# Row pair two in seven products in the first feed-forward block of a two-layer trunk

## The chip, the cores and the metric

The kernel runs on one core of one Trainium2 chip. The metric is device time in microseconds of one execution, as a median over runs; "the profiled execution" is a single one of them, taken by the hardware profiler.

## The reference

A decoder trunk of two layers works on 256 tokens of 2048 features in fp32. Layer 0 mixes tokens with a chunkwise mLSTM, layer 1 with a Griffin recurrent block; after each mixer stands a feed-forward part, which alone is touched here:

```python
def swiglu(x, w_in, w_out):
    g, u = jnp.split(x @ w_in, 2, axis=-1)
    return (jax.nn.silu(g) * u) @ w_out
...
        h = h + mix
        h = h + swiglu(rms_norm(h, norm_ffn[layer]), ffn_w_in[layer], ffn_w_out[layer])
    return rms_norm(h, norm_final)
```

`w_in` is 2048 x 11264 (gate and up halves of 5632 columns each), `w_out` is 5632 x 2048.

## The kernel before, in words

**Precision.** An fp32 matrix is split into an upper part (a cast to fp32r on ACT, `whi` for weights) and a lower part (raw minus upper on DVE, `wlo`). A product of two matrices is three matmuls, upper by upper, upper by lower and lower by upper (`product`, lines 821, 822 and 823). The names of the tiles carry the case: `whi`/`wlo` for a plain pair, `whix`/`wlox` and `whit`/`wlot` for one in seven products, `whio`/`wloo` for output weights, `p_f` and `m_f` for split activations.

**Tiling of the feed-forward part.** The columns of each half of `w_in` are taken in 11 blocks of 512 (`j` = 0 to 10, block one is `j` = 0). Within a block the 2048 rows of `w_in` are taken in 8 pairs of 128-row tiles (`p` = 0 to 7, so pair number two is `p` = 1). A pair makes a 2 x 2 problem: two token blocks of 128, two row tiles, and two column blocks (gate and up). It is done in one of two ways:

- plain: 8 products, into four PSUM banks named Q5, P2, Q3 and P4;
- in seven products of sums and differences (Strassen's scheme), into the same four banks and three more, P1, P7 and Q6. The weights' side then needs sums of the raw tiles first: `sum` at lines 314, 317 and 318, then the split of three raw tiles (`whix`, `wlox`) and of four sums (`whit`, `wlot`). The activations' side has its seven combinations ready in `p_f`.

Each bank sums over all pairs of the block. P1, P7 and Q6 get their last product at `p` = 6; then line 855 copies P1, line 856 subtracts that from Q6, and line 858 subtracts P7. After `p` = 7 lines 861 to 870 finish the block. The order of the seven products is P1, P2, Q3, Q5, P7, Q6, P4.

Which pairs are plain is said by three constants:

```python
SEVENS = (1, 2, 3, 4, 5, 6)
BOTH = (1, 2, 3, 4)
SECOND = (3,)
    def is_plain(j, p):
        return p not in SEVENS or j == 0 and p in BOTH or j == 1 and p in SECOND
```

**Activations.** `NormPairs.pair(p)` turns a pair of feature tiles of `h` by four transposes on PE (`tr_f`, line 467) into a bank that `misc` hands out, scales it on ACT into a tile `c` (line 471), takes differences on DVE (line 473 for `p` = 0 and 7, lines 477 to 480 for the others) and splits the result into `p_f`. A pair in `BOTH` is prepared for both ways: one copy (line 490), one difference (line 491) and one split into `m_f` more. Pairs 0 to 5 are prepared beside the output projection of the mixer. Pairs 6 and 7 are left over as pending work, and are run in block one after `p` = 0 and after `p` = 1:

```python
            if left == 0 and p < 2:
                run_pending()
```

In the feed-forward part `misc` takes the banks in turn, one buffer each: `misc=["P1", "Q6", "P7"]`. The `c` tiles of pairs 6 and 7 share one place, `raw0` of the pool `rawo`, with a raw tile of output weights.

**Buffers and queues.** Raw weights come by DMA on SP's queue (line 305, two loads of 512 KB for a pair) into three places in rotation, and `whi` and `wlo` have three places each; in block one the second raw tile and the second `whi` tile have an extra place. A planner orders the instructions of each engine ahead of time by priority and readiness; weight sums, splits and the work on finished banks are raised by `AHEAD` = 1000. A tile whose place is still held waits for the last reader of the tile before it. The products with `w_out` (`outs`) for a block are spread over the next one, so block one has none.

Of the kernel before, what the change touches and what calls it, by code (L numbers as in the profile page):

```python
# [28 lines left out]

SEVENS = (1, 2, 3, 4, 5, 6)  # L30

BOTH = (1, 2, 3, 4)

SECOND = (3,)

# [9 lines left out]
def kernel(  # L45
# [247 lines left out]
    def is_plain(j, p):  # L293
        return p not in SEVENS or j == 0 and p in BOTH or j == 1 and p in SECOND

# [157 lines left out]
    class NormPairs(Norm):  # L453
# [6 lines left out]
        def pair(self, p):  # L460
# [26 lines left out]
            self.x.append(xt)  # L487
            if p in BOTH:

# [721 lines left out]
```

## Time and profile before

| | |
|---|---|
| median of 3 runs | 2078.71 us (2077.93 to 2078.84) |
| profiled execution | 2078.14 us |
| its span | 2076.0 us |
| granted TensorE clock, mean | 0.999 |
| matmuls on PE | 10490 |
| moved from HBM | 401.84 MB |

Times in the profile count from the start of the span. PE is TensorE's matmuls and PEld its weight loads, DVE is VectorE, ACT is ScalarE, SP the queue that issues the DMAs. In rows of a timeline stand the start, the duration, engine, line, operation, output tile and input tiles with buffer numbers left out, and in brackets the idle time before it with what ended it. A `P` or `Q` as an output is one of the banks above. In rows of a table of stretches stand the busy times of PE, PEld, DVE, ACT and POOL with their counts of instructions, then the granted clock, the DMA engines' share and GB/s. Groups of instructions show total busy time, the mean in ns and the idle time before them. Block one of layer 0 runs from about 398 to 441 us, that of layer 1 982 us later.

### The profile page before, as it was taken

The numbers are of one execution on the slowest core, as the hardware profiler recorded it, in microseconds if no ns is written. First come the engines' busy times: TensorE is split into PE (matmuls) and PEld (weight loads), VectorE is DVE, ScalarE is ACT, GpSimd is POOL, SyncE is SP. The second block draws the span as 40 slices with busy tenths as digits, with TensorE's granted clock in tenths as the row PEclk, the third lists the DMA queues.
The fourth block names the chain that finished last, engine by engine and source line by source line (L and its number), as shares of the span: only waits on it lengthen the run. The fifth ranks groups of instructions, "written<-read, shape, count | busy, mean of one in ns | idle before, by whom it ended". The sixth has DMA issues, their size and how long they took to land.

```text
span 2076.0 us, 27538 instructions
## 1 busy us (share of the span) xinstructions
PE 2066.2 (100%) x10490; PEld 1755.4 (85%) x10490; DVE 1733.4 (83%) x1888; ACT 1343.1 (65%) x1623; POOL 43.3 (2%) x62
## 2 busy tenths in 40 slices
PE   9999999999999999999999999999999999999998
PEld 8988888888888888888889999888888888888886
DVE  6655556699999999999976787679999999999995
ACT  6345446566777677767764778556776776776774
POOL 0011110000000000000000000000000000000002
PEclk9999999999999999999999999999999999999999
DMA  7556656555665566665555666665666556566653
GB/s 229 172 159 178 181 177 227 185 199 190 210 214 197 186 222 203 203 213 196 182 180 159 191 190 185 218 215 183 203 213 213 202 187 210 199 209 211 203 191 133
DMA packets 211900, 405.74 MB, mean 195 GB/s; under 512 B 15080, under 2 KB 15800, under 8 KB 211640
## 3 DMA queue, kind: packets, MB, share of 16 engines
q1 hardware_dynamic: 211048, 402.92, 59.2%
q8 instruction: 82, 1.34, 0.3%
q10 hardware_dynamic: 720, 1.07, 0.2%
q14 instruction: 50, 0.41, 0.1%
HBM read 401.84 MB, written 2.10 MB: 195 GB/s over the span
## 4 chain that ended last, share of the span: by engine, by line
PE 96%; DVE 2%; ACT 1%; issue 1%; DMA 0%; POOL 0%; ACTq 0%; POOLq 0%; DVEq 0%
PE P L821 7%; PE out L821 7%; PE P L823 7%; PE P L822 7%; PE out L823 7%; PE out L822 7%; PE Q L821 6%; PE Q L822 6%; PE Q L823 6%; PE po L332 3%; PE po L330 3%; PE po L331 3%; PE v L330 1%; PE o L332 1%; PE v L331 1%; PE rec L349 1%
## 5 line engine op out<-in xcount | busy, mean ns | idle before, releaser
L246 DVE TENSOR_TENSOR wlo<-raw,whi 128x1024 fp32r<-128x1024 f32 (+1 forms) x226 | 273.4, 1213 | 171.4 <-ACT whi L245 168.9
L245 ACT CAST whi<-raw 128x1024 fp32r<-128x1024 f32 (+1 forms) x226 | 234.7, 1043 | 196.2 <-PE po L332 42.6
L270 ACT CAST whit<-sum 128x1024 fp32r<-128x1024 f32 x244 | 251.4, 1052 | 147.4 <-DVE sum L318 77.6
L271 DVE TENSOR_TENSOR wlot<-sum,whit 128x1024 fp32r<-128x1024 f32 x244 | 292.2, 1218 | 20.4 <-ACT whit L270 20.3
L821 PE MATMUL out<-whio,hh 128*128 128x512 f32 x704 | 274.9, 391 | 0.1
L822 PE MATMUL out<-wloo,hh 128*128 128x512 f32 x704 | 274.0, 389 | 0.0
L823 PE MATMUL out<-whio,hh 128*128 128x512 f32 x704 | 273.9, 389 | 0.0
L270 ACT CAST whio<-rawo 128x1024 fp32r<-128x1024 f32 (+1 forms) x166 | 183.6, 1106 | 61.8 <-PE out L823 52.8
L271 DVE TENSOR_TENSOR wlox<-raw,whix 128x1536 fp32r<-128x1536 f32 x122 | 213.7, 1751 | 10.7 <-ACT whix L270 10.6
L271 DVE TENSOR_TENSOR wloo<-rawo,whio 128x1024 fp32r<-128x1024 f32 (+1 forms) x166 | 209.6, 1281 | 3.1 <-ACT whio L270 2.7
L270 ACT CAST whix<-raw 128x1536 fp32r<-128x1536 f32 x122 | 181.0, 1484 | 33.8 <-DMA raw<-in_ffn_w_in_dram 18.9
L940 ACT COPY h<-out 128x512 f32<-128x512 f32 x154 | 90.1, 585 | 128.4 <-PE out L823 128.2
L821 PEld LDWEIGHTS out<-whio,hh 128*128 128x128 f32 x704 | 132.2, 188 | 29.3 <-ACT out L929 1.6
L314 DVE TENSOR_TENSOR sum<-raw 128x1024 f32<-128x1024 f32 x122 | 149.1, 1222 | 8.8 <-DMA raw<-in_ffn_w_in_dram 3.8
L823 PEld LDWEIGHTS out<-whio,hh 128*128 128x128 f32 x704 | 132.2, 188 | 27.6
L822 PEld LDWEIGHTS out<-wloo,hh 128*128 128x128 f32 x704 | 132.2, 188 | 27.1
L271 DVE TENSOR_TENSOR wlo<-raw,whi 128x2048 fp32r<-128x2048 f32 x54 | 122.0, 2288 | 30.0 <-ACT whi L270 30.0
L270 ACT CAST whi<-raw 128x2048 fp32r<-128x2048 f32 x54 | 101.2, 1913 | 18.0 <-DMA raw<-in_ffn_w_in_dram 17.8
L821 PE MATMUL P<-whix,p_f 128*128 128x512 f32 x244 | 96.6, 397 | 0.1
L929 ACT COPY out<-h 128x512 f32<-128x512 f32 x156 | 91.9, 589 | 6.4 <-DVE h L938 4.6
L822 PE MATMUL Q<-wlot,p_f 128*128 128x512 f32 x244 | 95.1, 390 | 0.0
L822 PE MATMUL P<-wlox,p_f 128*128 128x512 f32 x244 | 95.1, 390 | 0.0
(293 smaller groups left out, 5028.4 us busy)
## 6 DMA issues: line engine op xcount, KB each, us to landing
raw<-in_ffn_w_in_dram SPq DMA_DIRECT2D x352, 512.0 KB, 4.6
rawo<-in_ffn_w_out_dram SPq DMA_DIRECT2D x176, 512.0 KB, 4.8
raw<-in_m_w_in_dram SPq DMA_DIRECT2D x94, 512.0 KB, 3.8
raw<-in_r_w_in_dram SPq DMA_DIRECT2D x64, 512.0 KB, 4.2
raw<-in_m_w_out_dram SPq DMA_DIRECT2D x32, 512.0 KB, 3.7
raw<-in_r_w_out_dram SPq DMA_DIRECT2D x32, 512.0 KB, 4.4
gr<-in_r_gate_w_dram SPq DMA_DIRECT2D x8, 512.0 KB, 3.8
out_dram<-y SPq DMA_DIRECT2D x4, 512.0 KB, 3.0
```

The lines of the kernel that those rows point to most:

```text
L245: nc.scalar.copy(hi[:, i:i + step, 0:ncols], r)
L246: nc.vector.tensor_tensor(lo[:, i:i + step, 0:ncols], r, hi[:, i:i + step, 0:ncols].bitcast(F32), op=ALU.subtract)
L270: nc.scalar.copy(hi, src)
L271: nc.vector.tensor_tensor(lo, src, hi.bitcast(F32), op=ALU.subtract)
L314: nc.vector.tensor_tensor(t[:, 0:2, :], raw[:, 1:3, :], raw[:, 3:4, :].broadcast_to([P, 2, NB]), op=ALU.add)
L330: nc.tensor.matmul(o, lhsT=ah[:, bs], rhs=hi, start=(k == 0), stop=False)
L331: nc.tensor.matmul(o, lhsT=ah[:, bs], rhs=lo, start=False, stop=False)
L821: nc.tensor.matmul(o, lhsT=a[0], rhs=b[0], start=start, stop=False, **kw)
L822: nc.tensor.matmul(o, lhsT=a[0], rhs=b[1], start=False, stop=False, **kw)
L823: nc.tensor.matmul(o, lhsT=a[1], rhs=b[0], start=False, stop=stop, **kw)
L929: nc.scalar.copy(o, hs)
L940: nc.scalar.copy(hs, o)
```

## The change

`BOTH` loses its first entry. So in block one of each layer pair number two (`p` = 1) is taken in seven products, as it is in the other blocks, and `pair(1)` no longer prepares what the plain way needs.

```diff
 SEVENS = (1, 2, 3, 4, 5, 6)
 
-BOTH = (1, 2, 3, 4)
+BOTH = (2, 3, 4)
 
 SECOND = (3,)
```

## The prediction

> **What bounds the kernel now.** I read the page first: busy times, then the chain that ended last.
>
> ```profile
> span 2076.0 us, 27538 instructions
> PE 2066.2 (100%) x10490; PEld 1755.4 (85%) x10490; DVE 1733.4 (83%) x1888; ACT 1343.1 (65%) x1623; POOL 43.3 (2%) x62
> PE 96%; DVE 2%; ACT 1%; issue 1%; DMA 0%; POOL 0%; ACTq 0%; POOLq 0%; DVEq 0%
> ```
>
> PE has work in 2066.2 of 2076.0 us and is 96% of the chain. Fewer matmuls can pay; anything that makes PE wait costs its full length. Then the stretches around the first block of layer 0's feed-forward part (PE, PEld, DVE, ACT, POOL busy, granted clock), and one later in the layer:
>
> ```profile
> 404.00:410.00 6.00, 6.00 (x30) 4.92 (x30) 5.12 (x4) 4.47 (x5) 0.00 (x0) 1.00 0.55 193
> 436.00:441.00 5.00, 5.00 (x24) 4.14 (x23) 5.00 (x6) 2.97 (x3) 0.00 (x0) 1.00 0.90 304
> 1000.00:1060.00 60.00, 60.00 (x264) 49.11 (x263) 54.65 (x49) 43.54 (x48) 0.00 (x0) 1.00 0.55 182
> ```
>
> PE never stops, and DVE is full at the end of block one (5.00 of 5.00). The last row gives the price of a matmul on PE: 60.00 us / 264 = 0.227 us. (The 0.39 us of a single matmul overlaps with the next one.)
>
> **The change: PE work removed.** A plain pair takes 8 products, one in seven takes 7, and a product is 3 matmuls. So each layer loses 3 matmuls of 0.227 us, 0.68 us; both layers 1.36 us. That is 0.07% of 2078 us. It is the whole gain that is to be had: under 0.2%, about what a measurement of this kernel can tell from no change.
>
> **The weight side.** The pair's weights now need three sums and two splits instead of one split:
>
> ```profile
> L271 DVE TENSOR_TENSOR wlo<-raw,whi 128x2048 fp32r<-128x2048 f32 x54 | 122.0, 2288 | 30.0 <-ACT whi L270 30.0
> L270 ACT CAST whi<-raw 128x2048 fp32r<-128x2048 f32 x54 | 101.2, 1913 | 18.0 <-DMA raw<-in_ffn_w_in_dram 17.8 <-ACT whit L270 0.2
> L314 DVE TENSOR_TENSOR sum<-raw 128x1024 f32<-128x1024 f32 x122 | 149.1, 1222 | 8.8 <-DMA raw<-in_ffn_w_in_dram 3.8 <-DVE ds L856 1.6 <-issue 1.2
> L317 DVE TENSOR_TENSOR sum<-sum,raw 128x512 f32<-128x512 f32 x122 | 83.7, 686 | 1.4
> L270 ACT CAST whix<-raw 128x1536 fp32r<-128x1536 f32 x122 | 181.0, 1484 | 33.8 <-DMA raw<-in_ffn_w_in_dram 18.9 <-DVE ds L856 5.3 <-PE Q L823 5.0
> L271 DVE TENSOR_TENSOR wlox<-raw,whix 128x1536 fp32r<-128x1536 f32 x122 | 213.7, 1751 | 10.7 <-ACT whix L270 10.6
> L270 ACT CAST whit<-sum 128x1024 fp32r<-128x1024 f32 x244 | 251.4, 1052 | 147.4 <-DVE sum L318 77.6 <-DVE sum L314 43.2 <-PE Q L823 26.4
> L271 DVE TENSOR_TENSOR wlot<-sum,whit 128x1024 fp32r<-128x1024 f32 x244 | 292.2, 1218 | 20.4 <-ACT whit L270 20.3
> ```
>
> DVE: 1.22 + 2 x 0.69 + 1.75 + 2 x 1.22 - 2.29 = +4.5 us a layer. ACT: 1.48 + 2 x 1.05 - 1.91 = +1.7 us. Where does it fall? The pair's raw weights are there at 395.2, when ACT casts them:
>
> ```profile
> 395.18 1.91 ACT L270 CAST whi<-raw 128x2048 fp32r<-128x2048 f32 x1 [6.43 <-DMA raw<-in_ffn_w_in_dram]
> 397.05 0.69 DVE L531 TENSOR_TENSOR h<-po,h 128x512 f32<-128x512 f32 x1 [6.89 <-PE po L332]
> ```
>
> DVE idles 6.89 us up to 397.05, so the sums can start at 395.2. With the two h updates of L531 among them the DVE work (6.8 + 1.4 us) ends near 403.4; the pair's first product starts on PE at 403.73 (below), and the t half is wanted only three products, 2.0 us, later. I cost it at nothing. If that cover were gone, PE would wait for what sticks out, at most the added 4.5 us a layer.
>
> **The activation side of that pair** loses a copy, a difference and a split. They are the four rows below (of another such pair), 0.7 us of ACT and 0.7 us of DVE, beside the output projection, where PE is full: nothing on the path.
>
> ```profile
> 380.04 0.29 DVE L491 TENSOR_TENSOR c_f<-c_f 128x128 f32<-128x128 f32 x1
> 380.40 0.30 ACT L490 COPY c_f<-c_f 128x128 f32<-128x128 f32 x1
> 380.74 0.41 ACT L270 CAST m_f<-c_f 128x256 fp32r<-128x256 f32 x1
> 381.34 0.42 DVE L271 TENSOR_TENSOR m_f<-c_f,m_f 128x256 fp32r<-128x256 f32 x1
> ```
>
> **The queues and buffers.** No DMA is added. A seven takes one more whi and wlo tile, so the rotation moves by one; the loads that wait on SP until a split has read a raw tile move with the splits, by one at most (2.29 us). The DMA engines are 0.55 busy in the stretch from 404, so a late load is soon made up: I take 0, and what came of it would be a wait on weights, inside rival (c).
>
> **The PSUM banks.** This is the step that decides. Row pairs seven and eight (p = 6, 7) of the activations are turned inside block one, after products p = 0 and p = 1. Their transposes take the banks P1 and Q6, because `misc` hands out P1, Q6, P7 in turn:
>
> ```profile
> 403.38 0.60 PE L467 MATMUL tr_f<-ident,h 128*128 128x128 f32 x4
> 403.73 0.48 PE L821 MATMUL Q<-whi,p_f 128*128 128x512 f32 x1
> 407.64 0.83 ACT L471 ACTIVATE c_f<-tr_f,cols 128x256 f32<-128x256 f32 x2
> 409.31 0.60 PE L467 MATMUL tr_f<-ident,h 128*128 128x128 f32 x4
> 418.41 0.84 ACT L471 ACTIVATE c_f<-tr_f,cols 128x256 f32<-128x256 f32 x2
> ```
>
> Before, nothing else needs these banks until p = 5, since p = 0 to 4 are plain and use only Q5, P2, Q3 and P4. After the change p = 1 opens P1, P7 and Q6 and holds them to p = 6. So:
>
> P1: the product of p = 1 must wait until ACT has read p = 6's transposes, 407.64 + 0.83 = 408.5 above. The other six products fill 403.73 + 6 x 0.68 = 407.8, so if that one goes last PE waits 0 to 0.7 us; ACT has one split less ahead of that read if p = 4's moves behind it, so I take 0.
>
> Q6: it now belongs to p = 1's sum when p = 7's transposes (409.31) want it, and comes free only when L856 has read the finished sum after p = 6. Those transposes move from 409 to 436, just ahead of the products of p = 7 that need them. Queued behind that wait on PE is everything that follows: p = 7 ends the sums of the block, and block two needs their banks. The rows there now:
>
> ```profile
> 434.76 0.39 PE L823 MATMUL Q<-whit,p_f 128*128 128x512 f32 x1
> 435.67 0.39 PE L821 MATMUL Q<-whi,p_f 128*128 128x512 f32 x1
> 435.34 0.68 DVE L856 TENSOR_TENSOR ds<-Q,ds 128x512 f32<-128x512 f32 x1
> 435.94 2.28 DVE L271 TENSOR_TENSOR wlo<-raw,whi 128x2048 fp32r<-128x2048 f32 x1
> 438.14 0.68 DVE L858 TENSOR_TENSOR ds<-ds,P 128x512 f32<-128x512 f32 x1
> ```
>
> Q6's last matmul starts at 434.76, L856 ends at 436.02, and PE starts p = 7 at 435.67 with no pause. The chain from transposes to a usable activation can be read where it is short, at pair one (p = 0):
>
> ```profile
> 333.46 0.60 PE L467 MATMUL tr_f<-ident,h 128*128 128x128 f32 x4
> 334.09 0.84 ACT L471 ACTIVATE c_f<-tr_f,cols 128x256 f32<-128x256 f32 x2
> 335.21 0.42 DVE L473 TENSOR_TENSOR c_f<-c_f 128x256 f32<-128x256 f32 x1
> 335.66 0.83 ACT L270 CAST p_f<-c_f 128x768 fp32r<-128x768 f32 x1 [0.73 <-DVE c_f L473]
> 336.53 0.96 DVE L271 TENSOR_TENSOR p_f<-c_f,p_f 128x768 fp32r<-128x768 f32 x1 [0.90 <-ACT p_f L270]
> ```
>
> 0.63 + 0.84 + 0.42 + 0.83 with short hops is 2.8 us to the end of the cast. With both engines free PE restarts at 436.1 + 2.8 = 438.9: low end, 438.9 - 435.67 = 3.2 us, less 0.35 for the transposes' own PE time (403.38 to 403.73), which is paid already: 2.9. But DVE is in the split of 435.94 until 438.2, then L858 to 438.75; L473 then ends at 439.2 and the cast at 440.1: 440.1 - 435.67 - 0.35 = 4.1 us. High end: one more big split ahead of it (2.28): 6.4. The lower half of the activation (0.96) is hidden: each product has two matmuls that need only the upper half, 16 x 0.227 = 3.6 us of work to put first. I take 4.1, because DVE is full in 436 to 441 (above), and the splits are given priority over this chain. PE has little else: block two's products need Q5, P2, Q3 and P4, held by p = 7; two matmuls of its p = 1 into P1 could fit, 0.45 us, which takes the low end to 2.4.
>
> Pair eight's c tile shares its place with the output weights' raw tile, whose load now waits for it:
>
> ```profile
> 422.57 6.87 SPq L910 DMA_DIRECT2D rawo<-in_ffn_w_out_dram  x2
> 452.94 0.39 PE L821 MATMUL out<-whio,hh 128*128 128x512 f32 x1
> ```
>
> It moves to about 441 and is first used at 452.94, later still after the stall: hidden; without that cover it would cost the load's few microseconds.
>
> Layer 1 repeats this 982.0 us later, L856 on the same beat:
>
> ```profile
> 1417.34 0.69 DVE L856 TENSOR_TENSOR ds<-Q,ds 128x512 f32<-128x512 f32 x1
> ```
>
> **Sum.** 2 x 4.1 - 1.36 = +6.8 us. The profiled execution took 2078.14 us (span 2076.0 and 2.1 around it), 0.6 under the median of 2078.71: 2085.0 against itself, 2085.5 against the median. With 2.4 and 6.4 a layer: 2082.1 and 2090.1.
>
> **Where a rule speaks.** The row first: the last matmul starts at 2068.34, and the granted clock of the last stretch is 0.81.
>
> ```profile
> 2068.34 0.39 PE L823 MATMUL out<-whio,hh 128*128 128x512 f32 x1
> 2070.00:2076.00 6.00, 0.00 (x0) 0.00 (x0) 1.15 (x2) 1.33 (x2) 0.34 (x1) 0.81 0.44 175
> ```
>
> 0.81 over 6 us is full clock until 2073.7 and half after it: here the clock fell 5 us after PE's last work. My stall is under 4 us and broken by the transposes, so the sum has no slow matmuls. By the Trainium skill, "TensorE: Matmul & The Clock Gate", Part 1, an idle window of about 3.4 us halves the clock and another busy one restores it; the trace agrees that it falls after idling, at a later point.
>
> **The rivals.** (a) No stall, faster by 1.4 us, 2077.3: p = 7's transposes get Q6 before p = 1's product into it. This needs PE idle around 404 to 407 so that later work is pulled ahead; PE is 6.00 of 6.00 there, and product 6 comes before the transposes in the order of the code. Against me: the h rows are ready by then. This is the rival on the other side; it decides once the four transposes issue ahead of p = 1's Q6 product. (b) The stall is there but short, under 2.7 us a layer: 2078.7 to 2082.8. For it: 2.4 is the low end above. (c) The added DVE work is not hidden: 3.8 us a layer net of the 0.7 saved, 2 x 3.8 - 1.36 = +6.2, 2084.9, with PE waiting at p = 1 and 2 instead. Against it: the 6.89 us of idle DVE. (d) The stall and a fall of the clock: half speed for as long as the fall took to come, 5 us, loses 2.5 us a layer: 2085.5 + 5 = 2090.5. Against it: the 5 us at the end.
>
> **Chances.** My forecast 0.62, (a) 0.16, (b) 0.08, (c) 0.06, (d) 0.08. Slower by over 0.2% (4.2 us): forecast, (c), (d), 0.76. Within 0.2%: (a) and (b), rounded, 0.23. Faster by over 0.2%: 0.01, since 1.36 us is all there is. The likeliest case alone is 2082 to 2090; to leave out no more than 2 in 10 the range reaches down to (a) and up past (d): 2077 to 2091.
>
> **What would show it.** L821, L822 and L823 lose two matmuls each, one a layer. The second `tr_f` group of each layer stands after L856 near 436 instead of near 409, and PE has a gap of about 4 us before p = 7, ended by the cast of `p_f`; its twin lies 982 us later. `sum`, `wlox` and `wlot` appear between 395 and 403. Wrong if the group stands near 404 to 409, or if PE's gap lies at p = 1 or 2, or if PE shows no gap at all.

## The result and the profile after

The changed kernel takes 2098.85 us (median of 4 runs, 2098.46 to 2100.51) beside 2078.61 us of the kernel before in the same job: ratio 1.0099, interval 1.0082 to 1.0117. It is 20.2 us slower. The forecast was 2085.5 us, in a range of 2077 to 2091: the direction was right, the size a third of what came.

The page of the profile after, its span and busy times:

```profile
span 2096.9 us, 27535 instructions
PE 2073.0 (99%) x10484; PEld 1757.6 (84%) x10484; DVE 1741.1 (83%) x1894; ACT 1344.4 (64%) x1623; POOL 45.3 (2%) x62
```

PE has its six matmuls less (10484 for 10490), yet its busy time rose by 6.8 us. Work that takes longer with fewer instructions points to slower matmuls, and the table of stretches shows where (us, then PE, PEld, DVE, ACT, POOL busy, granted clock, DMA share, GB/s):

```profile
404.00:411.00 7.00, 5.37 (x25) 4.13 (x24) 6.90 (x9) 4.12 (x7) 1.79 (x1) 1.00 0.35 90
436.50:444.30 7.80, 2.56 (x9) 1.12 (x8) 7.51 (x9) 3.04 (x4) 0.00 (x0) 0.87 0.76 269
444.30:449.40 5.10, 5.10 (x13) 4.01 (x14) 2.15 (x2) 0.00 (x0) 0.00 (x0) 0.53 0.81 262
449.40:457.50 8.10, 8.10 (x37) 6.67 (x36) 6.60 (x8) 5.50 (x6) 0.00 (x0) 1.00 0.08 31
```

Three places in block one of layer 0 (layer 1 has the same three 992 us later): PE loses 1.6 us between 404 and 411; it works 2.56 of 7.80 us between 436.5 and 444.3; and then it does 13 matmuls in 5.10 us at a clock of 0.53, where the next stretch does 37 in 8.10. At that later rate 13 take 2.85 us, so 2.2 us are lost there.

The first place, in rows of the timeline (start, duration, engine, line, output and inputs, idle time before and what ended it):

```profile
402.73 0.68 DVE L531 TENSOR_TENSOR h<-po,h 128x512 f32<-128x512 f32 x1
403.47 0.66 PE L467 MATMUL tr_f<-ident,h 128*128 128x128 f32 x4
405.37 1.90 ACT L270 CAST whi<-raw 128x2048 fp32r<-128x2048 f32 x1
407.17 0.82 ACT L471 ACTIVATE c_f<-tr_f,cols 128x256 f32<-128x256 f32 x2
408.04 0.50 PE L821 MATMUL P<-whix,p_f 128*128 128x512 f32 x1 [1.63 <-ACT c_f L471]
```

Pair two's product into P1 waits until ACT has read pair seven's transposes out of that bank; ACT does that at 407.17, behind a cast of 1.90 us. The second h update on DVE is now behind the new sums and ends at 403.41, so the transposes wait for it by 0.25 us (0.65 in layer 1).

The second place, PE, then ACT, then DVE:

```profile
436.28 0.39 PE L823 MATMUL P<-whit,p_f 128*128 128x512 f32 x1
436.88 0.66 PE L467 MATMUL tr_f<-ident,h 128*128 128x128 f32 x4 [0.22 <-DVE ds L856]
438.23 0.50 PE L821 MATMUL P<-whix,p_f 128*128 128x512 f32 x1 [0.69 <-ACT whix L270]
442.48 0.80 PE L822 MATMUL P<-wlox,p_f 128*128 128x512 f32 x1 [3.75 <-DVE wlox L271]
444.29 0.80 PE L821 MATMUL Q<-whi,p_f 128*128 128x512 f32 x1 [0.58 <-ACT p_f L270]
443.40 0.83 ACT L270 CAST p_f<-c_f 128x768 fp32r<-128x768 f32 x1 [4.49 <-DVE c_f L473]
436.15 0.68 DVE L856 TENSOR_TENSOR ds<-Q,ds 128x512 f32<-128x512 f32 x1
436.75 2.28 DVE L271 TENSOR_TENSOR wlo<-raw,whi 128x2048 fp32r<-128x2048 f32 x1
438.94 0.68 DVE L858 TENSOR_TENSOR ds<-ds,P 128x512 f32<-128x512 f32 x1
439.54 1.22 DVE L314 TENSOR_TENSOR sum<-raw 128x1024 f32<-128x1024 f32 x1
440.68 1.75 DVE L271 TENSOR_TENSOR wlox<-raw,whix 128x1536 fp32r<-128x1536 f32 x1
442.35 0.69 DVE L317 TENSOR_TENSOR sum<-sum,raw 128x512 f32<-128x512 f32 x1
442.95 0.42 DVE L473 TENSOR_TENSOR c_f<-c_f 128x256 f32<-128x256 f32 x1
```

The transposes of pair eight stand behind L856, as forecast. But the difference L473 runs at 442.95, not at 438.75: behind L858 stand three operations for block two's weights (1.22 + 1.75 + 0.69), and ACT idles 4.49 us for it. PE starts p = 7 at 444.29. Without a stall it would have started 0.227 + 0.35 us after 436.28, at 436.86: a gap of 7.4 us, of which three matmuls of block two fill 0.68.

The sum per layer: -0.68 (three matmuls) + 0.45 (late transposes, mean of the layers) + 1.8 (P1; the matmul's start is 1.8 us later than a free PE gives) + 6.75 (Q6, net) + 2.2 (slow matmuls) = 10.5, for both layers 21.0 against 20.9 us between the two spans.

### The profile page after: what moved, and what is told of

Read it like the earlier page. It is cut to its first block, busy times and chain, and to the rows that moved or that the text cites. A ratio compares the mean times of both kernels' runs of the same rounds, so it can differ in the third digit from the quotient of the medians.

```text
span 2096.9 us, 27535 instructions
## 1 busy us (share of the span) xinstructions
PE 2073.0 (99%) x10484; PEld 1757.6 (84%) x10484; DVE 1741.1 (83%) x1894; ACT 1344.4 (64%) x1623; POOL 45.3 (2%) x62
## 3 DMA queue, kind: packets, MB, share of 16 engines
q10 hardware_dynamic: 720, 1.07, 0.2%
## 4 chain that ended last, share of the span: by engine, by line
PE 97%; DVE 1%; ACT 1%; issue 0%; POOL 0%; ACTq 0%; POOLq 0%; DVEq 0%
PE out L821 8%; PE out L823 8%; PE out L822 8%; PE P L821 7%; PE P L822 7%; PE P L823 7%; PE Q L821 6%; PE Q L822 6%; PE Q L823 6%; PE po L332 3%; PE po L330 3%; PE po L331 3%; PE qk L349 1%; PE qk L347 1%; PE qk L348 1%; PE o L332 1%
## 5 line engine op out<-in xcount | busy, mean ns | idle before, releaser
L271 DVE TENSOR_TENSOR wlot<-sum,whit 128x1024 fp32r<-128x1024 f32 x248 | 297.6, 1221 | 23.3 <-ACT whit L270 23.3
L271 DVE TENSOR_TENSOR wlo<-raw,whi 128x2048 fp32r<-128x2048 f32 x52 | 117.5, 2289 | 31.6 <-ACT whi L270 31.6
L821 PE MATMUL P<-whix,p_f 128*128 128x512 f32 x248 | 98.9, 399 | 4.6 <-ACT c_f L471 3.3
L823 PE MATMUL P<-whix,p_f 128*128 128x512 f32 x248 | 97.1, 392 | 0.0
L821 PE MATMUL P<-whit,p_f 128*128 128x512 f32 x248 | 96.9, 391 | 0.0
```

The costliest lines, as they stand in the source:

```text
L271: nc.vector.tensor_tensor(lo, src, hi.bitcast(F32), op=ALU.subtract)
L821: nc.tensor.matmul(o, lhsT=a[0], rhs=b[0], start=start, stop=False, **kw)
L823: nc.tensor.matmul(o, lhsT=a[1], rhs=b[0], start=False, stop=stop, **kw)
```

## The experiments

Two theories were set against each other from the trace: **banks** (the transposes of pairs seven and eight have to share P1 and Q6 with pair two's sums) and **weights side** (the added 4.5 us of DVE work a layer delay the weights). What follows names each by its label; differences are to the kernel before, timed in the same job (2078.5 to 2078.8 us).

**e4_late_alone: the stall without the change.** The kernel before, with pair two plain; only the place moves where pair eight is prepared:

```diff
-            if left == 0 and p < 2:
+            if left == 0 and p == 0 or left == 0 and p == 6:
                 run_pending()
```

> The kernel before (p = 1 plain, no added weight sums), with pair eight's pending work run after p = 6 instead of after p = 1; the bank of its transposes is Q6 as ever. Theory B: lateness alone costs what the changed kernel lost before p = 7: gap of about 7 us plus about 2.5 us of half clock a layer, 2 x 9.3 = +18.5, about 2097. Theory W: p = 1's weights are as before, so about 2079; a gap of up to 3 us a layer at most, 2085.

2094.24 us, +15.7 (ratio 1.0073, 1.0058 to 1.0089), 2.8 below the 2097 of the bank theory and far above the 2085 of the other. The same picture as in the changed kernel, again with L473 late on DVE (441.70, its transposes at 435.64), and 10.2 us at half clock:

```profile
441.70 0.42 DVE L473 TENSOR_TENSOR c_f<-c_f 128x256 f32<-128x256 f32 x1
443.04 0.80 PE L821 MATMUL Q<-whi,p_f 128*128 128x512 f32 x1 [0.58 <-ACT p_f L270]
```
```profile
438.50:448.70 10.20, 6.89 (x15) 4.96 (x16) 6.54 (x8) 0.83 (x1) 0.00 (x0) 0.50 0.82 285
```

So some 16 of the 20 us come from when pair eight is prepared, with none of the seven-product work of pair two there.

**e1_both_out, e2_p7_out, e3_p6_out: another bank.** The changed kernel, with the transposes of both left-over pairs, of pair eight alone, or of pair seven alone in the spare bank `out`, which block one does not use:

```diff
-            pt = misc(f"tr_{self.name}{p}")
+            if named and p in (6, 7):   # e2: p == 7, e3: p == 6
+                named["misc"].append(named["misc"].pop(0))
+                pt = pool_of("out").tile([P, NB], F32, tag="out", name=f"tr_{self.name}{p}")
+            else:
+                pt = misc(f"tr_{self.name}{p}")
```

> The change, with the transposes of row pairs seven and eight put into the PSUM bank of the output products, which block one does not use, in place of P1 and Q6; nothing else. Theory B (banks): all that was lost is the wait for P1, the wait for Q6 and what the Q6 wait does to the clock. Then PE has no gap at p = 1 or before p = 7, the clock stays at 1.00, and the time is before - 1.36 + at most 0.9 (two short waits of pair seven's transposes for the updated h rows): 2077.2 to 2078.2. Theory W (weights): the 4.5 us more of DVE work a layer cause the loss; then this stays near the changed kernel, 2095 to 2100, since the DVE work is the same.

> The change, with only row pair eight's transposes (p = 7) in the bank of the output products; pair seven's stay in P1. Theory B: the wait for Q6 and the half clock are gone, the wait of about 1.8 us for P1 at p = 1 stays in both layers: before + 2 x (1.8 + 0.3 - 0.68) = about +3, 2081 to 2082. Theory W: near 2095 to 2100.

> The change, with only row pair seven's transposes (p = 6) in the bank of the output products; pair eight's stay in Q6. Theory B: the P1 wait is gone, the late transposes, the gap of about 7 us before p = 7 and the half clock stay: changed kernel - 2 x 1.8 = about 2095. Theory W: near 2099.

e3 (P1 freed): 2094.81, +16.3 (1.0063 to 1.0090): the 1.8 us a layer of P1 are gone (first row below: 7.00 of 7.00), 4 us less than the change; the stall and the half clock stay (second row). e2 (Q6 freed): 2082.77, +4.3 (1.0011 to 1.0029): the stall and the half clock are gone, P1's wait stays (third row); it is 0.8 us over what was expected, and its trace has one more wait, 1.0 us at p = 6 of layer 0. e1 (both freed): 2083.83, +5.3 (1.0014 to 1.0034).

```profile
404.00:411.00 7.00, 7.00 (x33) 5.67 (x32) 6.64 (x6) 6.06 (x8) 1.79 (x1) 1.00 0.30 83
441.20:448.00 6.80, 6.12 (x14) 4.35 (x15) 3.50 (x5) 0.83 (x1) 0.00 (x0) 0.50 0.78 267
```
```profile
408.07 0.51 PE L826 MATMUL P<-whix,p_f 128*128 128x512 f32 x1 [1.59 <-ACT c_f L476]
```

The banks hold the large part. But e1 missed: with neither bank in the way it should have been faster than before, and it is not. Its eight runs differ in their granted clock: three at 0.999 take 2081.49 to 2082.01 us (the profiled one is among them), five at 0.997 or 0.998 take 2082.91 to 2086.02. So some 3.4 us of the 5.3 are there without a fall of the clock (2081.95 against 2078.51), and e1 is no slower than e2, whose runs are all at 0.999. The profiled run has a wait at p = 6 in both layers, 2.0 and 2.6 us (PE, then ACT, DVE and SP's issue; L915 is L910 of the other kernels):

```profile
432.94 0.50 PE L827 MATMUL P<-wlox,p_f 128*128 128x512 f32 x1 [1.29 <-DVE wlox L271]
428.66 1.06 ACT L270 CAST whio<-rawo 128x1024 fp32r<-128x1024 f32 x1 [3.25 <-DMA rawo<-in_ffn_w_out_dram]
429.62 1.48 ACT L270 CAST whix<-raw 128x1536 fp32r<-128x1536 f32 x1
429.75 1.22 DVE L271 TENSOR_TENSOR wloo<-rawo,whio 128x1024 fp32r<-128x1024 f32 x1 [0.18 <-ACT whio L270]
424.57 6.80 SPq L915 DMA_DIRECT2D rawo<-in_ffn_w_out_dram  x2
```

In the kernel before the same chain ran 2 us earlier:

```profile
422.57 0.37 SPq L910 DMA_DIRECT2D rawo<-in_ffn_w_out_dram  x1
426.73 1.05 ACT L270 CAST whio<-rawo 128x1024 fp32r<-128x1024 f32 x1 [3.33 <-DMA rawo<-in_ffn_w_out_dram]
```

The output weights' load waits for pair eight's `c` tile, whose place it takes; its cast stands ahead of p = 6's on ACT, its lower part ahead of p = 6's on DVE. That tile is let go 2 us later in e1. In the changed kernel that load goes out only after p = 7 has begun, so nothing of this shows there:

```profile
445.30 0.37 SPq L910 DMA_DIRECT2D rawo<-in_ffn_w_out_dram  x1
```

In e3, too, it goes out that late, and there PE has no wait at p = 6. Is that what is left of e1?

**e10_out_cplace, e11_out_cplace34, e12_before_cplace: the c tiles in another place.** e10 is e1 with

```diff
-            place, tag = ("c", "c") if "c" in pools else ("rawo", "raw0")
+            place, tag = ("c", "c") if "c" in pools else ("f", "h0")
```

e11 takes pair three in seven products as well, e12 makes this edit alone in the kernel before.

> The change with both left-over transposes in the spare bank (as e1) and, besides, the c tiles of pairs seven and eight in the place of the second raw tile (h0), which is free from about 403 to 446 us, instead of the place that the output weights' raw tile uses. Chain theory (what is left of e1, 5.3 us, comes of the shared place: p_f of pair eight read two us later, the output weights' load two us later, its cast and its lower part ahead of p = 6's on ACT and DVE): the load of L910 is issued near 420 again or earlier, no wait at p = 6 (2.0 us in layer 0 and 2.6 in layer 1 in e1), time 2078.5 - 1.4 + up to 1 for the late transposes of pair seven (0.2 and 0.65) = 2077.2 to 2078.2. Rival (the weights side alone is late by the added 4.5 us of DVE and stays late): the waits at p = 6 stay, 2083.8.

> As e10, and pair number three (p = 2) in seven products as well (BOTH = 3, 4). PE loses another 2 x 3 x 0.227 = 1.4 us. If the weights side is hidden: 2075.8 to 2077. Rival: the second 4.5 us of DVE a layer, in a stretch where DVE had 5.12 of 6.00 us already, makes PE wait for sums or lower parts from p = 2 on: 2079 to 2084, with PE gaps ended by wlox or wlot between 404 and 430 us. I hold the rival for likelier.

> The kernel before with only the c tiles of pairs seven and eight moved to the place of the second raw tile. Control for e10: there the output weights' load came early enough already (422.57 us), so the move alone should give nothing: 2077.5 to 2079.5. If it gains more than 1.5 us, e10's gain over e1 isn't the mending of a delay that the change made.

2110.36 (+31.7), 2103.17 (+24.5) and 2123.35 us (+44.7): all three missed, and for a reason that says nothing of the theory. `h0` is also where block one's second raw tile goes, and pair seven's `c` tile is asked for first in the order of the code; so the raw tile's load, which goes out by 393 us in the kernel before, now waits for pair seven. In e10, SP's issue and the wait on PE (it is 9.52 us in e11, where the load goes out at 407.95, and 20.11 in e12):

```profile
409.81 0.88 SPq L305 DMA_DIRECT2D raw<-in_ffn_w_in_dram  x2
418.25 1.22 PE L826 MATMUL P<-whix,p_f 128*128 128x512 f32 x2 [12.76 <-ACT whix L270]
```

I had gone by when the place is free, not by who asks for it first: the very mechanism of the change, made again.

**e13_c8_place, e16_c8_place34: only pair eight's tile moved**, which stands behind that raw tile in the order of the code; e16 with pair three in seven too.

```diff
-            place, tag = ("c", "c") if "c" in pools else ("rawo", "raw0")
+            place, tag = ("c", "c") if "c" in pools else ("rawo", "raw0") if p == 6 else ("f", "h0")
```

> As e1 (both left-over transposes in the spare bank), and only pair eight's c tile moved to the place h0, where it stands behind the second raw tile in the order of the code (in e10 pair seven's c tile came ahead of that raw tile and held back its load). Pair seven's c tile stays in raw0 of rawo, so the output weights' load waits for pair seven alone. Chain theory: the load of L910 that e1 issued at 424.57 us goes out before 421, the casts whio and wloo are done before p = 6's raw tiles land, the waits at p = 6 (2.0 and 2.6 us) go: 2077.2 to 2078.2. Partly: 2078.2 to 2081 if whio and wloo, which stay ahead of p = 6's casts in ACT's and DVE's order, still cost their own 1.05 + 1.23 us there. Rival (weights late for another reason): 2083.8.

> As e13, and pair number three (p = 2) in seven products too, to see whether a second pair pays. Hidden weights side: 1.4 us under e13. Rival, which I hold for likelier: DVE's next 4.5 us a layer make PE wait between 404 and 435 us, 1 to 6 us over e13.

e13: 2080.18 us, +1.4 (ratio 1.0008, 0.9999 to 1.0017), where e1's runs at the same clock of 0.999 are at +3.4. The load goes out at 420.16, the cast `whio` at 424.94, and of e1's 2.0 and 2.6 us at p = 6 there remain 0.5 and 0.9:

```profile
420.16 0.37 SPq L915 DMA_DIRECT2D rawo<-in_ffn_w_out_dram  x1
431.56 0.50 PE L827 MATMUL P<-wlox,p_f 128*128 128x512 f32 x1 [0.32 <-DVE wlox L271]
```

That is the case "partly" of the expectation. The shared place was most of what was left of e1: the waits at p = 6 fall from 4.6 to 1.4 us. What remains in e13 (0.25 and 0.65 of late transposes, 0.5 and 0.9 at p = 6, 2.3 us) is more than the 1.36 us saved, by 0.9; measured are 1.4, in an interval that still takes in no change.

Why does `wlox` still come late? The next raw tiles go out at 409.49 instead of 405.52, and DVE idles 2.45 us for them; behind them stand pair eight's difference and split and `wloo` (2.6 us together). In e3 the tiles are as late (2.56 us), but those three do not stand there: its `wlox` runs at 427.30 instead of 429.76, and PE does not wait. So both are needed for the wait, as far as these traces tell; no run takes the late tiles away.

e16: 2093.80, +15.0 (1.0060 to 1.0085): a second pair does not pay. It is 13.6 us over e13, where 1 to 6 were expected. Its raw tiles land late and PE waits for a lower part, at p = 3, 6.13 us in layer 0 and 5.25 in layer 1; behind both waits the clock is at half speed for 6.83 us:

```profile
418.54 1.22 DVE L314 TENSOR_TENSOR sum<-raw 128x1024 f32<-128x1024 f32 x1 [4.57 <-DMA raw<-in_ffn_w_in_dram]
422.02 0.79 PE L827 MATMUL Q<-wlo,p_f 128*128 128x512 f32 x1 [6.13 <-DVE wlo L271]
```

The wait was foreseen, its cause not: DVE is not full there but idle for 4.57 us, behind a sum whose tile has not landed, with `wlo` queued behind that sum.

**e5_chain_first: DVE's order.** The changed kernel, with pair eight's chain raised like the weights' work:

```diff
-                self.pair(2 * q + 1)
+                with ExitStack() as raised:
+                    if named:
+                        raised.enter_context(tc.high_priority(offset=AHEAD))
+                    self.pair(2 * q + 1)
```

> The change, with all of pair eight's chain (transposes, scaling, difference, split) raised by AHEAD like the weights' sums and splits, so that on DVE its difference L473 need not stand behind wlo, L858, sum, wlox and sum. If that order makes the stall long: L473 straight after L856 or the split in progress, PE waits 3 to 4.5 us instead of 7 (436.5 to about 440), the clock falls for little or not at all, 2098.8 - 2 x (3 + 2) = 2086 to 2091. Rival (the chain waits for ACT or for PSUM whatever DVE does): 2096 to 2099.

Median 2087.95 us (+9.2; 1.0037 to 1.0064). L473 now follows the split in progress, and p = 7 starts 3.4 us after the transposes instead of 7.4:

```profile
437.15 0.66 PE L467 MATMUL tr_f<-ident,h 128*128 128x128 f32 x4 [0.22 <-DVE ds L859]
438.49 0.50 PE L824 MATMUL P<-whix,p_f 128*128 128x512 f32 x1 [0.69 <-ACT whix L270]
440.56 0.79 PE L824 MATMUL Q<-whi,p_f 128*128 128x512 f32 x1 [1.56 <-ACT p_f L270]
437.01 2.28 DVE L271 TENSOR_TENSOR wlo<-raw,whi 128x2048 fp32r<-128x2048 f32 x1
439.21 0.43 DVE L473 TENSOR_TENSOR c_f<-c_f 128x256 f32<-128x256 f32 x1
```

Three of its four runs take 2087.54 to 2088.14 us at a mean granted clock of 0.999, the fourth 2093.57 at 0.996. The fourth is the profiled one; in it the clock fell in both layers.

**e6_fill, e15_fill_behind: the half clock.** The changed kernel, with 18 idle matmuls into the spare bank to keep PE busy while it waits for pair eight; in e15 they are ordered behind the transposes:

```diff
+            if named and p == 7:
+                fill = pool_of("out").tile([P, NB], F32, tag="out", name=f"fill_{self.name}")
+                x6 = self.x[6][:, 0]
+                with after(turn_i):   # e15 only; turn_i: the last transpose
+                    for i in range(18):
+                        nc.tensor.matmul(fill, lhsT=x6[:, 0, :], rhs=x6[:, 0:4, :].rearrange("p n t -> p (n t)"),
+                                         start=True, stop=True, skip_group_check=True)
```

> The change, with 18 matmuls of 128 x 512 more into a bank that nobody reads, right behind the transposes of pair eight, so that PE is busy while it waits for that pair's activations. It leaves the wait for Q6 and the chain behind the transposes as they are. If the half clock is a cost of its own, 2.6 us a layer: granted clock 1.00 in the stretch from 444 to 450, time 2098.8 - 5 = 2093.5 (2092.5 to 2095). If the slow matmuls hide in other waits: unchanged, 2098.8. If the filling itself is on the path: over 2099.

> e6 mended: in e6 the 18 idle matmuls stood ahead of the transposes of pair eight, in PE's full stretch, and cost their own 2 x 4.1 us. Here they are ordered behind the last of the four transposes, into a bank that nobody reads, so they fill PE's wait for pair eight's activations (436.5 to 444.3 us). Clock theory: granted clock 1.00 where it was 0.5 (6.8 us in layer 0, 10.2 in layer 1), p = 7's matmuls 0.227 us apart instead of 0.427, 2.6 us a layer less than the change: 2098.8 - 5.2 = 2093.6 (2092.5 to 2095). Rival (the half clock is hidden by other waits): 2098.8.

e6: 2106.76, 8 us over the change. The idle matmuls stood ahead of the transposes, in a full stretch, and cost 2 x 18 x 0.227 = 8.2; it tells nothing of the clock. e15: 2095.70 us (2094.64 to 2097.59; +16.9). The wait is as long as in the change (in layer 0 p = 7 starts 7.4 us after the transposes, at 445.61), but there the clock holds:

```profile
444.50:450.00 5.50, 4.43 (x20) 3.62 (x20) 3.58 (x5) 0.92 (x2) 0.00 (x0) 1.00 0.70 238
1435.00:1440.50 5.50, 4.43 (x13) 3.53 (x13) 2.62 (x4) 0.83 (x1) 0.00 (x0) 0.69 0.66 230
```

In layer 1 of the profiled run, the slowest of the four, it still fell, for 3.4 us (last row: 13 matmuls where layer 0 did 20). The fastest run is 4.2 us under the change, the median 3.2; 5.2 were expected. So slow matmuls were a cost of their own, about 2 us a layer, and filling PE gets most of it back.

## Why the prediction was wrong in size

**PE work removed, and weights side.** The six matmuls are gone, as worked out. The weights side was "at nothing" by a start of the sums at 395.2. They started at 397.58 behind the first h update, and the second update then fell behind them: the added work was not on the weights' path at p = 1 but delayed the transposes by 0.25 and 0.65 us. In the changed kernel these 0.9 us are all that shows of the weights side; in e13, with the banks out of the way, the waits come to 2.3 us over both layers, more than the 1.36 us saved. The loads, put at 0, move by 3.4 us (405.52 to 408.95), more than the 2.29 allowed for; in the changed kernel no wait of PE comes of it, in e13 it has a part in the waits at p = 6. I weighed one engine's idle time, and not the order in which its work would stand.

**P1.** Taken as 0, bounds 0 to 0.7; measured 1.8 a layer (e3: 4.0 us for both). ACT's read was about where the sum had it: it ends at 407.99, against 408.5, though the cast of 1.90 us still stands ahead of it. What failed is "if that one goes last": PE comes to P1's product at 406.25, and in its order the rest of P7, Q6 and P4 stands behind it.

**Q6.** The step that decided was right in its mechanism and place (e2 and e4). Its size was not: 4.1 us a layer forecast, 7.4 measured. The forecast put L473 behind one split and L858; the three weight operations of block two were left out, though the text itself said that splits are given priority over this chain and put one more at the high end, 6.4. e5 shows that this is DVE's order: raised, the gap is 3.4 us, near the 2.9 of the low end's chain.

**The clock.** Slow matmuls were put at nothing and cost 2.2 us a layer. Rival (d), at 0.08, had the right mechanism. I held it off by the end of the run: the clock fell 5 us after the last work, so a stall "under 4 us" (4.1 by my own sum) would not do it. That reading was the mistake, and the last section shows what the clock goes by.

**The output weights' load** was "hidden" in the changed kernel, as said (p = 7's delay moved the first use too), but it is not free: with the stall gone it is most of what made e1 miss; in five of e1's eight runs a lower granted clock adds to it.

**The sum.** Forecast -0.68 + 4.1 = 3.4 us a layer; measured 10.5: 2.25 more at P1 and the transposes, 2.65 more at Q6 (net of block two's matmuls), 2.2 from the clock. The direction was right because the wait for Q6 was. Its measured size alone would have given 2078.7 + 2 x 6.75 - 1.36 = 2090.8 us, still inside the range; what was put at nothing, P1 with the late transposes and the slow matmuls, took the time out of it. No version here beats the kernel before: the best that can be had is 1.36 us, and e13 comes to 1.4 us slower, not clear of no change.

## What to carry to other kernels

Before taking a resource for longer, list who else asks for it in the order of the code, and what that one's late turn queues up behind on every in-order engine: the price was 7.4 us and not the bare chain's 2.8, because of DVE's queue. A saving on the bound engine that adds work on a nearly full engine is worth at most the saving (here 0.07%), so the risk decides. And a wait on PE can cost twice: its length, and the slow matmuls behind it.

## What the runs showed of the hardware

The clock does not wait for PE to be idle for long. The half-speed stretches in these traces last 6.83 us (the change, layer 0; e3; e5), 10.24 (the change, layer 1; e4, layer 0) and 3.41 (e15), all multiples of 3.413, and in each run the falls lie whole multiples of that apart. Cut into such windows, of the change and (last three rows) of e5:

```profile
404.73:408.14 3.41, 1.78 (x9) 1.16 (x7) 3.31 (x5) 3.26 (x4) 1.79 (x1) 1.00 0.13 11
438.86:442.27 3.41, 0.00 (x0) 0.00 (x0) 3.41 (x4) 0.05 (x1) 0.00 (x0) 1.00 1.02 375
442.27:445.68 3.41, 2.62 (x5) 1.66 (x6) 2.66 (x5) 0.83 (x1) 0.00 (x0) 0.50 0.44 138
445.68:449.09 3.41, 3.41 (x9) 2.64 (x8) 1.23 (x1) 0.00 (x0) 0.00 (x0) 0.50 0.98 333
```
```profile
405.57:408.98 3.41, 1.77 (x8) 1.16 (x7) 3.35 (x3) 2.68 (x4) 1.79 (x1) 1.00 0.18 40
436.29:439.70 3.41, 1.80 (x8) 0.79 (x6) 3.41 (x5) 2.41 (x5) 0.00 (x0) 1.00 0.61 168
439.70:443.11 3.41, 2.56 (x6) 2.07 (x7) 3.41 (x5) 0.80 (x1) 0.00 (x0) 0.50 1.00 371
```

A window with little PE work is followed by half speed, and half speed ends after a window in which PE was busy throughout (3.41) or nearly so (3.17 in e12 is the least); 2.62, 2.56 and, in e10, 2.92 were not enough. In e5 the fall came after a window with 1.80 us of PE work, and the longest pause of PE there was 1.56 us (rows of e5 above), 0.71 of it inside the window. In e15's layer 1 it came after 1.73 us of work, and with no pause over 1.07 (a row of the table, then the row of that pause):

```profile
1433.56:1436.98 3.42, 1.73 (x7) 1.06 (x7) 3.13 (x5) 0.83 (x1) 0.00 (x0) 1.00 0.56 200
1436.08 0.50 PE L828 MATMUL Q<-whi,p_f 128*128 128x512 f32 x1 [1.07 <-ACT p_f L270]
```

Windows with 1.77 and 1.78 us elsewhere were followed by no fall, so busy time alone does not say where the bound lies: those windows held 8 or 9 wide matmuls, the one of e5 four wide ones and the four narrow transposes. Where the grid lies against the stall differs from run to run, which would explain why e5 and e1 have runs with and without a fall, and e5's 5.8 us between them (2093.57 against 2087.77); only one run of each set was traced, so that is argued and not shown.

By the Trainium skill, "TensorE: Matmul & The Clock Gate", Part 1, the window is 3413 ns long and free-running: the traces agree, and it explains the 5 us at the end of the kernel before (counted back from the fall at 2073.75, the window up to 2070.34 still had 1.80 us of PE work, and only the next one had none). The same page of the Trainium skill, in "Why this matters for your kernels", asks for no idle gaps of PE over about 3 us between matmul bursts: here shorter ones were enough for a fall, 1.56 us at most in e5 and 1.07 in e15.
